# Low parts of the gates' inputs on VectorE, six branches' products with the state on GpSimd, another order of units, and another start, in a decoder trunk on one core

## The chip, the cores and the metric

The kernel runs on one core of a Trainium2 chip. The metric is the device time of one execution in microseconds (us); the kernel before takes 1247.46 us, the median of three runs between 1246.99 and 1248.34.

The engines are called TensorE (PE in the profile; its weight loads are PEld), VectorE (DVE), ScalarE (ACT), GpSimd (POOL) and SyncE (SP), which issues nearly all loads. Each engine works through its own instructions strictly in their order.

## The reference, cut to what matters

The trunk has two layers over 512 prompt tokens and 8 x 8 sample tokens, width 1024. Layer 0 is the recurrent block; the rest of the kernel (two feed-forward parts, shared keys and values, sliding attention, final norm) isn't touched.

```python
sh1, sc1, g1, ... = split(silu(c) @ ada_w + ada_b)          # modulation, from the condition c
h = rms_norm(x, g) * (1 + sc1) + sh1
xr, yg = split(h @ w_in)                                    # two branches, 8 blocks of 128 each
xr = causal_dwconv(xr, conv_buf, conv_w, conv_b)            # width 4
r, i = sigmoid(einsum(xr blocks, gate_w) + gate_b)          # the gates, block by block
a = exp(8 * r * log_sigmoid(lambda))
state_t = a * state_(t-1) + sqrt(1 - a * a) * (i * xr)      # the scan over the tokens
out = (state * gelu(yg)) @ w_out
x = x + g1 * out
```

## The kernel before, in words

**Tokens and blocks.** The tokens are two halves h of 288 columns (256 prompt and 32 sample tokens). Feature blocks c of 128 lie on the partitions. A product with a weight of 128 x 1024 is 8 blocks, and each block is three matmuls, because every operand is held as a high part (rounded to fp32r) and a low part (the rest): high x high, high x low, low x high. Raw weights come by DMA into `raw` tiles; ScalarE casts the high part and VectorE subtracts for the low part, both into `wh` tiles.

**The recurrent block.** The string `RNN` lists its units: `x3` is the branch that is convolved for block 3 (`evac_xr`), `g3` its gates (`gates`), `y3` its gelu branch (`evac_yg`). In `gates`, ScalarE casts the convolved input to its high part (tile `ta`), and line 1180 takes the low part (tile `tb`): 128 x 300, by GpSimd. Six matmuls follow (two gates, three each); the tanh and exp of ScalarE, five products of VectorE and a scan of VectorE then give the state in `s0`. GpSimd puts start values into the scan's operands (`ta<-shT`, `sl<-tb`, a memset) and copies ends out (`ho`). In `evac_yg`, ScalarE takes gelu, VectorE multiplies by the state (lines 1244 and 1245: 256 prompt columns, then 32 sample columns), ScalarE casts the high part, VectorE takes the low part; both wait as `sl` tiles for the product with `w_out`.

**What sets the order.** The code doesn't issue instructions itself. A `Recorder` writes every operation down with its operands, and `schedule` (line 235) then places all of them on the five engines, with a planned cost for each, and emits them in the order of the planned starts. So a change of one operation's engine or of a constant moves many rows, on every engine. That is also why all instructions have one line, L497, in the profile: it is the line that emits. `early(n)` makes what it encloses more urgent; `rec.hold` makes what follows wait for the writers of a tile.

**The start.** SyncE loads x (five tiles of rows, `reg`), the conditions c (`raw`), two vectors and then weights. `x_half` takes the sums of squares, whose by-product goes to spare `raw` tiles, and turns x with transposes. `keep_busy` offers 60 transposes of the unit matrix to TensorE for the time in which it would have nothing to do. `more_vectors` loads eight small vector groups from GpSimd's queue, `vectors_rest` turns them with four transposes. `lambdas` turns the decay parameters, and `decay_rates` makes two tiles (`sp`, `nsp`) from them with some 27 small operations of GpSimd, placed after the block pair `DKC`. `ada_first` makes the first modulation in four steps of two blocks, each from 2 MB of `ada_w`.

Of the kernel before, what the change touches and what calls it, by code (L numbers as in the profile page):

```python
# [15 lines left out]
AF = mybir.ActivationFunctionType  # L16
ALU = mybir.AluOpType
AX = mybir.AxisListType

P = 128  # L20
D = 1024
# [5 lines left out]
HP = 256  # L27
HC = 288
CW = 300
# [26 lines left out]
QUAD = (3, 4, 5, 6)  # L56
QK = 2
YT = lambda td, ta, sl: td
RNN = "x0 x1 x2 x3 x4 x5 g0 g1 y0 y1 g2 x6 g3 y2 y3 g4 y4 g5 x7 y5 g6 g7 y7 y6"
ATT = "q0A q2A a0A q1A q0B a2A q1B q3A a0B q2B q4A a1A a1B a4A a3A q3B a2B q5A q4B a3B q6A a5A q5B q7A a6A a4B s0A a5B s1A s2A s3A q6B q7B a7A s0B s1B a6B fA a7B o0A s2B s3B o1A o2A fB"  # L60
LOOK = {"PE": 24, "DVE": 24, "ACT": 24, "POOL": 24, "SP": 24}
NRAW = 4
FILL = 250
DKC = 2
XB = 100
AF_ = (1, 2, 2, 2)
NSL, NTA, NTB, NTD = 37, 7, 8, 4


SH1, SC1, G1, SH2, SC2, G2 = range(6)  # L70
# [68 lines left out]
class Recorder:  # L139
# [95 lines left out]
    def schedule(self):  # L235
# [22 lines left out]
        pos = {n: j for k in self.order for j, n in enumerate(self.order[k])}  # L258
        used = {n for n in last}
        table = [next(j for j, (n, _) in enumerate(TABLES) if n == "silu")]  # L260
        dma_free = [0.0]
        out = []

        def push(op):
# [35 lines left out]
        while n_left:  # L300
# [24 lines left out]
            for e in engs:  # L325
# [4 lines left out]
                for pr, i, op in avail[e]:  # L330
# [13 lines left out]
                    s = max(f, op.ready, at)  # L344
                    if op.port == 1:
                        s = max(s, port - 100 + (60 if holder == e else 0))
                    if e == "PE" and op.mode != mode:
                        s = max(s, f + 100)
# [19 lines left out]
            _, s, op, sw = best  # L368
# [24 lines left out]
            if op.lat:  # L393

                free[e] = s + op.cost
                b = max(s + op.cost + 650, dma_free[0])
                dma_free[0] = b + op.lat
                op.end = b + op.lat + (1700 if op.i >= self.strict else 1000)
            else:
                op.end = free[e] = s + cost  # L400
            for n in op.tiles:
# [122 lines left out]
def trunk_kernel(ctx, tc, a):  # L524
# [17 lines left out]
    def aux():  # L542
        return ps()
# [36 lines left out]
    @contextmanager  # L580
    def early(n):

        rec.bias -= n
        yield
        rec.bias += n
# [10 lines left out]
    v1, v2, v3, v4, v5, v6 = [s.f[:, 0:P] for s in vb]  # L596
    lam_ = sl()
    lam = lam_.f[0:8, 0:P]
    G.dma_start(lam, a["rnn_lambda"][0].rearrange("(r p) -> r p", p=P))

    def first_vectors():
        Q.dma_start(v1[0:96, :], a["ada_b"].rearrange("l (r p) -> (l r) p", p=P))
        Q.dma_start(v6[0:32, :], a["norm_g"].rearrange("l n (r p) -> (l n r) p", p=P))

    def more_vectors():
        G.dma_start(v2[64:80, :], a["kv_ada_b"].rearrange("(r p) -> r p", p=P))
        G.dma_start(v2[0:8, :], a["kv_norm_g"].rearrange("(r p) -> r p", p=P))
        G.dma_start(v2[8:40, :], a["rnn_conv_w"][0].rearrange("w (r p) -> (w r) p", p=P))
        G.dma_start(v2[40:48, :], a["rnn_conv_b"][0].rearrange("(r p) -> r p", p=P))
        G.dma_start(v2[48:64, :], a["rnn_gate_b"][0].rearrange("n (r p) -> (n r) p", p=P))  # L610
        G.dma_start(v3[0:96, :], a["state_conv"][0, 0:4].rearrange("b w (r p) -> (b w r) p", p=P))
        G.dma_start(v4[0:96, :], a["state_conv"][0, 4:8].rearrange("b w (r p) -> (b w r) p", p=P))
        G.dma_start(v5[0:64, :], a["state_h"][0].rearrange("b (r p) -> (b r) p", p=P))

    more_vectors()

    xt = [None] * 5

# [2 lines left out]
    def x_load(t):  # L621
        xt[t] = regs()
        if t < 4:
            Q.dma_start(xt[t].f, a["x_prompt"][0, t * P : (t + 1) * P, :])
        else:
            Q.dma_start(xt[t].f[0:64, :], a["x_sample"].rearrange("b t d -> (b t) d"))
# [17 lines left out]
        xt[t].done()  # L644

    S.activation(tst[1][:, 3:4], ones, AF.Silu)
    x_load(4)
    Q.dma_start(c9.f[0:1, :], a["c_prompt"])
    Q.dma_start(c9.f[1:9, :], a["c_sample"])
    for t in (0, 1):  # L650
        x_load(t)
    first_vectors()


    for q in range(2):
        S.activation(cst[q], cst[q], AF.Silu)
    pt = aux()
    for k in range(KC):
        T.transpose(pt[:, k * 16 : k * 16 + 9], cst[k // 4][:, (k % 4) * P : (k % 4) * P + P], ident[0:9, 0:9])
# [38 lines left out]
    def lambdas():  # L698
        pt = aux()
        T.transpose(pt[:, 0:8], lam, ident[0:8, 0:8])  # L700
        V.tensor_copy(lamT, pt[:, 0:8])
        lam_.done()
# [140 lines left out]
    def v48(t):  # L843
        return t.rearrange("p (b t) -> p b t", b=4)
# [329 lines left out]
    def gates(c):  # L1174
        def run(h):
            s1 = RN[h][c]
            xc = s1.f[:, 0:CW]
            xh, xl = ta(F32R), tb(F32R)
            S.copy(xh.r[:, 0:CW], xc)
            G.tensor_tensor(xl.r[:, 0:CW], xc, xh.f[:, 0:CW], ALU.subtract)  # L1180
            os_ = []
            for t in range(2):
                o = ps()[:, 0:CW]
                hi, lo = ug[c // 4].block(c % 4 * 2 + t)
                T.matmul(o, hi, xh.r[:, 0:CW], start=True, stop=False)
                T.matmul(o, lo, xh.r[:, 0:CW], start=False, stop=False)
                T.matmul(o, hi, xl.r[:, 0:CW], start=False, stop=True)
                os_.append(o)
            xh.done()
            xl.done()  # L1190

            s0, sa = sl(), sl()
            RN[h][c] = s0
            r_, i_ = ta(), tb()
            r, i, t, b = [y.f[:, 0:CW] for y in (r_, i_, s0, sa)]
            S.activation(r, os_[0], AF.Tanh, bias=hgb[:, 2 * c : 2 * c + 1], scale=0.5)
            S.activation(i, os_[1], AF.Tanh, bias=hgb[:, 2 * c + 1 : 2 * c + 2], scale=0.5)
            S.activation(t, r, AF.Tanh, bias=sp2[:, c : c + 1], scale=sp2[:, c : c + 1])
            S.activation(b, r, AF.Exp, bias=nsp4[:, c : c + 1], scale=nsp4[:, c : c + 1])
            V.scalar_tensor_tensor(xc, i, 1.0, xc, ALU.add, ALU.mult)  # L1200
            S.activation(r, t, AF.Sqrt)
            V.scalar_tensor_tensor(i, b, 1.0, t, ALU.add, ALU.mult)
            V.scalar_tensor_tensor(r, r, 0.5, xc, ALU.mult, ALU.mult)
            V.scalar_tensor_tensor(r, b, 1.0, r, ALU.add, ALU.mult)
            G.tensor_scalar(b, i, -1.0, 1.0, ALU.mult, ALU.add)
            G.memset(pads(b), 0.0)
            G.tensor_copy(pads(r), shT[:, 4 * h : 4 * h + 4, c])
            V.tensor_tensor_scan(t, b, r, 0.0 if h == 0 else ho5[:, 0, c, 0:1], ALU.mult, ALU.add)
            r_.done()
            i_.done()  # L1210
            s1.done()
            sa.done()
            G.tensor_copy(ho5[:, h, c], s0.f[:, 249:304].rearrange("p (b t) -> p b t", t=11)[:, :, 6])
        return run
# [23 lines left out]
    def evac_yg(c):  # L1238
        def f(h, o):
            s0 = RN[h][c]  # L1240
            t = YT(td, ta, sl)()
            v = t.f[:, 0:HC]
            S.activation(v, o[:, 0:HC], AF.Gelu_apprx_tanh)
            V.tensor_tensor(v[:, 0:HP], v[:, 0:HP], s0.f[:, 0:HP], ALU.mult)
            V.tensor_tensor(v48(v[:, HP:HC]), v48(v[:, HP:HC]),
                            s0.f[:, 259:303].rearrange("p (b t) -> p b t", t=11)[:, :, 0:8], ALU.mult)
            RN[h][c] = sl(F32R), sl(F32R)
            split(RN[h][c][0].r[:, 0:HC], RN[h][c][1].r[:, 0:HC], v)
            s0.done()
            t.done()  # L1250
        return f
# [285 lines left out]
    def keep_busy(t, n):  # L1537
        with rec.when_idle():
            for i in range(n):
                T.transpose(t[:, 0:P], ident[:], ident[:])  # L1540
# [426 lines left out]

    def x_half(h):
        st = tst[h]
        for t in ((4, 0, 1), (2, 3))[h]:  # L1970

            w = raws()
            n, y = (64, tst[1][0:64, 2:3]) if t == 4 else (P, st[:, t % 2 : t % 2 + 1])
            src, dst = xt[t].f[0:n, :], w.f[0:n, :]
            if t % 2 == 0:
                S.activation(dst, src, AF.Square, accum_out=y)
            else:
                V.tensor_tensor_reduce(out=dst, in0=src, in1=src, op0=ALU.mult, op1=ALU.add, scale=1.0, scalar=0.0, accum_out=y)
            w.done()
            if t == 4:  # L1980
                V.tensor_scalar(tst[0][0:32, 2:3], y[0:32], 1.0 / D, EPS, ALU.mult, ALU.add)
                V.tensor_scalar(tst[1][32:64, 2:3], y[32:64], 1.0 / D, EPS, ALU.mult, ALU.add)
        V.tensor_scalar(st[:, 0:2], st[:, 0:2], 1.0 / D, EPS, ALU.mult, ALU.add)
        spread(h, 32 * h)
        for t in ((4, 0, 1), (2, 3))[h]:
            x_turn(t)


    keep_busy(aux(), 60)
    lambdas()  # L1990
    def load_one():
        load_more(nload[0] - nconv[0] + 1)

# [17 lines left out]
    for c in range(0, KC, 2):  # L2011
        ada_first(c, AF_[c // 2])
        for h in range(2):
            with early(E1):
                modulated(h, SC1, SH1, M1, slice(c, c + 2))
            if c + 2 == QK:
                quad_parts(h)
            if c == 0 and h == 0:
                with early(XB):
                    x_half(1)  # L2020
                rec.idle_end()
        if c == DKC:
            decay_rates()
    vectors_rest()
    first_norm[0] = False
# [130 lines left out]
```

## Time and profile before

| | |
|---|---|
| median of the runs | 1247.46 us |
| the profiled execution | 1247.53 us |
| its span | 1245.8 us |
| TensorE busy in the span | 1232.7 us, 9603 matmul records |
| VectorE, ScalarE, GpSimd busy | 895.3, 655.5, 461.9 us |
| loads | 160.85 MB read, 133 GB/s over the span |

The span runs from the first to the last instruction of the trace; the time has 1.7 us around it. A row of the timeline gives the start and the length in us, engine, line, operation, output<-input and shape, how many instructions are merged in it, and in brackets how long the engine had idled before and on what. A row of a group gives the number of instructions, their busy time in us and the mean of one in ns. A row of the waits gives the total, how often, and the longest.

### The profile page before, as it was taken

Reading aid. Unit: us, or ns where it says so; the run is one execution under the profiler, and the core shown is the slowest. Engines: PE = TensorE matmul, PEld = TensorE weight load, DVE = VectorE, ACT = ScalarE, POOL = GpSimd, SP = SyncE. Lnnn points to the kernel's source line nnn. Section 1 sums busy time; section 2 is a strip of 40 time slices with the busy share of each in tenths; the row PEclk is TensorE's granted clock in tenths of the full one; section 3 lists DMA queues with packets and bytes.
Section 4 is the critical chain, followed back from the end, with each engine's and each line's share of the span. In section 5 each row is a group of like instructions: output and inputs, shape, how many; then the busy total and the mean of one; then the engine's idle time right before and its main releaser. Section 6 shows DMA issues by size and latency. Waiting matters only on the chain.

```text
span 1245.8 us, 25395 instructions
## 1 busy us (share of the span) xinstructions
PE 1232.7 (99%) x9603; PEld 1171.4 (94%) x9603; DVE 895.3 (72%) x2141; ACT 655.5 (53%) x1462; POOL 461.9 (37%) x633
## 2 busy tenths in 40 slices
PE   8999999999999999999999999999999999999997
PEld 7888899999999999999999988999999999999997
DVE  5997885896675676477578888568767667747766
ACT  6778863852452454145367678448425435515533
POOL 4464340162441452246125445100426246335500
PEclk9999999999999999999999999999999999999999
DMA  9984644326556555444433321422332323323222
GB/s 317 298 266 162 197 150 153 124 73 216 170 184 203 172 169 166 162 145 155 119 88 69 72 61 41 122 75 99 98 105 69 110 78 102 102 83 87 84 87 77
DMA packets 221117, 165.41 MB, mean 133 GB/s; under 512 B 23757, under 2 KB 206025, under 8 KB 220962
## 3 DMA queue, kind: packets, MB, share of 16 engines
q1 hardware_dynamic: 220514, 163.45, 42.6%
q8 instruction: 76, 1.25, 0.4%
q14 instruction: 47, 0.39, 0.1%
q0 software_dynamic: 480, 0.32, 0.1%
HBM read 160.85 MB, written 4.87 MB: 133 GB/s over the span
## 4 chain that ended last, share of the span: by engine, by line
PE 94%; DMA 2%; DVE 2%; POOL 1%; ACT 1%; SPq 0%; issue 0%; DVEq 0%; POOLq 0%; ACTq 0%
PE mm L497 89%; PE ada L497 5%; DMA reg<-in_x_prompt_dram 1%; DVE wh L497 1%; DMA wh<-in_ada_w_dram 0%; DMA raw<-in_ffn_w_out_dram 0%; POOL tb L497 0%; SPq L497 0%; DVE ta L497 0%; DVE h L497 0%; POOL sl L497 0%; DMA wh<-in_cache_k_dram 0%; DVE tb L497 0%; ACT wh L497 0%; POOL ta L497 0%
## 5 line engine op out<-in xcount | busy, mean ns | idle before, releaser
L497 PE MATMUL mm<-h,wh 128*128 128x288 f32 x4080 | 583.5, 297 | 0.9 <-DVE h L497 0.4
L497 PEld LDWEIGHTS mm<-h,wh 128*128 128x128 f32 x4080 | 552.8, 188 | 11.2 <-issue 6.4
L497 PE MATMUL mm<-sl,wh 128*128 128x288 f32 x3237 | 464.6, 296 | 0.2 <-ACT sl L497 0.2
L497 PEld LDWEIGHTS mm<-sl,wh 128*128 128x128 f32 x3237 | 440.0, 188 | 6.8 <-issue 5.9
L497 ACT CAST wh<-raw 128x512 fp32r<-128x512 f32 (+3 forms) x394 | 270.6, 706 | 293.4 <-PE mm L497 182.9
L497 DVE TENSOR_TENSOR wh<-raw,wh 128x512 fp32r<-128x512 f32 (+3 forms) x396 | 360.5, 930 | 54.1 <-ACT wh L497 48.6
L497 POOL TENSOR_TENSOR raw<-raw 128x512 f32<-128x512 f32 x78 | 114.5, 1469 | 174.9 <-DVE wh L497 157.4
L497 DVE SCALAR_TENSOR_TENSOR x<-mm,mods,x 128x256 f32<-128x256 f32 x160 | 77.2, 483 | 122.8 <-PE mm L497 122.1
L497 POOL TENSOR_TENSOR x<-x,ta 128x32 f32<-128x32 f32 x120 | 42.1, 351 | 243.4 <-DVE ta L497 243.4
L497 POOL TENSOR_TENSOR raw<-raw,raw 128x512 f32<-128x512 f32 x78 | 116.1, 1488 | 4.6
L497 PE MATMUL mm<-tb,wh 128*128 128x288 f32 (+1 forms) x500 | 92.0, 299 | 2.4 <-POOL tb L497 2.4
L497 POOL TENSOR_TENSOR td<-td,td 128x288 f32<-128x288 f32 x39 | 32.7, 837 | 134.8 <-ACT td L497 121.7
L497 PEld LDWEIGHTS mm<-tb,wh 128*128 128x128 f32 x500 | 73.9, 188 | 6.3 <-POOL tb L497 2.9
L497 ACT ACTIVATE ta<-x 128x288 f32<-128x288 f32 (+1 forms) x56 | 24.4, 442 | 62.8 <-POOL x L497 39.9
L497 PE MATMUL mm<-ta,wh 128*128 128x288 f32 (+1 forms) x259 | 56.7, 296 | 0.0
L497 DVE TENSOR_TENSOR td<-mm,td 128x288 f32<-128x288 f32 x78 | 34.4, 453 | 22.7 <-PE mm L497 21.9
L497 PE MATMUL ada<-reg,cz 128*32 128x512 f32 (+1 forms) x408 | 47.2, 547 | 0.0
L497 DVE TENSOR_TENSOR sl<-td,sl 128x288 fp32r<-128x288 f32 x65 | 41.5, 642 | 7.9 <-ACT sl L497 7.6
L497 PEld LDWEIGHTS mm<-ta,wh 128*128 128x128 f32 x259 | 42.3, 188 | 1.0 <-ACT sl L497 0.8
L497 ACT ACTIVATE td<-td 128x288 f32<-128x288 f32 x39 | 17.3, 443 | 46.1 <-DVE td L497 46.1
L497 ACT ACTIVATE ta<-ta,stat 128x256 f32<-128x256 f32 (+2 forms) x72 | 32.5, 473 | 11.0 <-DVE stat L497 10.7
L497 ACT COPY ta<-mm 128x288 f32<-128x288 f32 (+1 forms) x51 | 19.1, 377 | 36.3 <-PE mm L497 35.2
(212 smaller groups left out, 1243.1 us busy)
## 6 DMA issues: line engine op xcount, KB each, us to landing
raw<-in_ffn_w_in_dram SPq DMA_DIRECT2D x88, 512.0 KB
reg<-in_ada_w_dram SPq DMA_DIRECT2D x72, 512.0 KB
raw<-in_ffn_w_out_dram SPq DMA_DIRECT2D x32, 384.0 KB
raw<-in_ffn_w_out_dram SPq DMA_DIRECT2D x32, 320.0 KB
reg<-in_kv_ada_w_dram SPq DMA_DIRECT2D x14, 512.0 KB
raw<-in_rnn_w_in_dram SPq DMA_DIRECT2D x13, 512.0 KB
wh<-in_ada_w_dram SPq DMA_DIRECT2D x24, 256.0 KB
raw<-in_rnn_w_out_dram SPq DMA_DIRECT2D x8, 512.0 KB
```

The costliest lines, as they stand in the source:

```text
L497: self.rec.add(eng, lambda: getattr(obj, name)(*map(real, args), **{k: real(v) for k, v in kw.items()}), cost, outs, ins, func, lat, port, ...
```

## The change: what it does

In `gates`, the low part of the input (line 1180) goes from GpSimd to VectorE: 16 operations of 128 x 300. In `evac_yg`, the products with the state of blocks 0 to 5 go from VectorE to GpSimd: 12 products of 256 columns and 12 of 32. The order of units in `RNN` is another. At the start: x tile 0 is loaded first instead of the samples; the eight vector groups and the decay parameters are loaded after the first modulation is written (`rec.hold`), not at once; the decay rates are made after the block pair 4 instead of 2; the by-product of the first squares goes into x of the other half; ScalarE gets one more early table load. In `schedule`, two planned costs of DMAs are others.

```diff
-RNN = "x0 x1 x2 x3 x4 x5 g0 g1 y0 y1 g2 x6 g3 y2 y3 g4 y4 g5 x7 y5 g6 g7 y7 y6"
+RNN = "x0 x1 x2 x3 x4 x5 g0 g1 y0 g2 y1 g3 y3 y2 x6 g4 x7 g5 y4 y5 g6 g7 y7 y6"
...
-DKC = 2
+DKC = 4
...
+NFILL = 60
+YG = 6
+OFF = 3000.0
...
-        dma_free = [0.0]
+        dma_free = [OFF]
...
+                if e == "POOL":
+                    op.end = s + op.cost + 5000
...
-    G.dma_start(lam, a["rnn_lambda"][0].rearrange("(r p) -> r p", p=P))
...
     def more_vectors():
+        G.dma_start(lam, a["rnn_lambda"][0].rearrange("(r p) -> r p", p=P))
...
-    more_vectors()
...
-    x_load(4)
+    x_load(0)
     Q.dma_start(c9.f[0:1, :], a["c_prompt"])
     Q.dma_start(c9.f[1:9, :], a["c_sample"])
-    for t in (0, 1):
-        x_load(t)
+    x_load(1)
+    x_load(4)
...
+    with early(1000):
+        S.activation(tst[0][:, 3:4], ones, AF.Sqrt)
...
-            G.tensor_tensor(xl.r[:, 0:CW], xc, xh.f[:, 0:CW], ALU.subtract)
+            V.tensor_tensor(xl.r[:, 0:CW], xc, xh.f[:, 0:CW], ALU.subtract)
...
-            V.tensor_tensor(v[:, 0:HP], v[:, 0:HP], s0.f[:, 0:HP], ALU.mult)
-            V.tensor_tensor(v48(v[:, HP:HC]), v48(v[:, HP:HC]),
+            E = G if c < YG else V
+            E.tensor_tensor(v[:, 0:HP], v[:, 0:HP], s0.f[:, 0:HP], ALU.mult)
+            E.tensor_tensor(v48(v[:, HP:HC]), v48(v[:, HP:HC]),
...
-            w = raws()
+            r = raws() if h else None
+            w = r.f if h else x[1].rearrange("p c n -> p (c n)")[:, D * (t % 2) : D * (t % 2 + 1)]
...
-    keep_busy(aux(), 60)
-    lambdas()
+    keep_busy(aux(), NFILL)
...
+                rec.hold = [mods[:, SC1, 0:2]]
+                more_vectors()
+                rec.hold = []
         if c == DKC:
+            lambdas()
             decay_rates()
```

TensorE, the start, before: the transposes of the unit matrix (`mm2`) stand between the others as they are planned. `reg1` is the sample tile, `reg2` and `reg3` are x tiles 0 and 1, `raw1` the conditions, `sl7` the decay parameters.

```order
L497 MATMUL mm2_99<-ident_66 128x128 x25
L497 MATMUL mm3_139<-ident_66,sl7_94 128x8
L497 MATMUL mm2_99<-ident_66 128x128 x2
L497 MATMUL mm5_149<-ident_66,reg1_97 128x64 x8
L497 MATMUL mm2_99<-ident_66 128x128 x7
L497 MATMUL mm1_179<-ident_66,raw1_105 128x9 x8
L497 MATMUL mm6_195<-ident_66,reg2_118 128x128 x4
```

TensorE, the same place after: here `reg1` and `reg2` are x tiles 0 and 1 and `reg3` is the sample tile.

```order
L503 MATMUL mm2_97<-ident_66 128x128 x50
L503 MATMUL mm4_178<-ident_66,reg1_94 128x128 x4
L503 MATMUL mm5_184<-ident_66,reg1_94 128x128 x4
L503 MATMUL mm2_97<-ident_66 128x128 x5
L503 MATMUL mm6_203<-ident_66,reg2_123 128x128
L503 MATMUL mm1_205<-ident_66,raw1_111 128x9 x8
```

50 of the 60 fillers now stand in a block at the front; 60 are planned in both. Further down, the turning of the decay parameters and of the vectors (`sl2` to `sl5`) has left the start and stands around the second step of the first modulation (`ada26` is its transpose, `ada27` the third step), after:

```order
L503 MATMUL ada26_586<-ident_66,ta8_536 128x128
L503 MATMUL mm32_588<-ident_66,sl2_352 128x80
L503 MATMUL mm33_590<-ident_66,sl3_431 128x96
L503 MATMUL mm33_590<-ident_66,sl4_446 128x96
L503 MATMUL mm33_590<-ident_66,sl5_461 128x64
L503 MATMUL ada27_601<-reg6_294,cz_78 32x128 x8
```

The same place before, where the third step follows at once:

```order
L497 MATMUL ada27_630<-ident_66,ta8_570 128x128
L497 MATMUL ada28_632<-reg6_324,cz_78 32x128 x8
L497 MATMUL ada28_632<-reg7_343,cz_78 32x128 x8
L497 MATMUL mm38_661<-h11_508,wh5_362 128x288
L497 MATMUL ada28_632<-reg8_355,cz_78 32x128 x8
```

What moved is four transposes, from a place among the fillers to one where the third step's modulation is due.

TensorE, a gate of the recurrent block, before: `ta47` is the high part of the input, `tb41` its low part, `mm74` and `mm76` other units.

```order
L497 MATMUL mm72_1797<-ta47_1779,wh27_1019 128x300
L497 MATMUL mm72_1797<-ta47_1779,wh28_1177 128x300
L497 MATMUL mm73_1803<-ta47_1779,wh27_1019 128x300
L497 MATMUL mm73_1803<-ta47_1779,wh28_1177 128x300
L497 MATMUL mm74_1808<-h01_375,wh41_1786 128x288 x2
L497 MATMUL mm72_1797<-tb41_1792,wh27_1019 128x300
L497 MATMUL mm73_1803<-tb41_1792,wh27_1019 128x300
```

TensorE, the gate of the same place after:

```order
L503 MATMUL mm72_1813<-ta47_1736,wh29_1133 128x300
L503 MATMUL mm72_1813<-ta47_1736,wh30_1149 128x300
L503 MATMUL mm72_1813<-tb41_1789,wh29_1133 128x300
L503 MATMUL mm73_1824<-ta47_1736,wh29_1133 128x300
L503 MATMUL mm73_1824<-ta47_1736,wh30_1149 128x300
L503 MATMUL mm73_1824<-tb41_1789,wh29_1133 128x300
```

The third matmul, which takes the low part, no longer stands behind matmuls of other units.

ScalarE, the first two gelu branches (`td11` and `td14`), after. The casts of `td11` and `td14` follow GpSimd's products, and tanh of gates (`ta36`, `ta38`) stand behind the casts:

```order
L503 ACTIVATE td11_1436<-mm49_1244 128x288
L503 ACTIVATE ta34_1442<-mm51_1330,hgb_81 128x300
L503 ACTIVATE tb30_1450<-mm52_1338,hgb_81 128x300
L503 ACTIVATE sl34_1457<-ta34_1442,sp2_79 128x300
L503 ACTIVATE td14_1463<-mm54_1382 128x288
L503 CAST sl31_1470<-td11_1436 128x288
L503 ACTIVATE ta36_1476<-mm55_1387,hgb_81 128x300
L503 ACTIVATE tb32_1482<-mm56_1460,hgb_81 128x300
L503 ACTIVATE sl39_1491<-ta36_1476,sp2_79 128x300
L503 CAST sl37_1501<-td14_1463 128x288
L503 ACTIVATE ta38_1505<-mm57_1467,hgb_81 128x300
```

Before, the same branches with the products by VectorE (`td11` and `td13`):

```order
L497 ACTIVATE td11_1359<-mm49_1249 128x288
L497 ACTIVATE td13_1386<-mm51_1340 128x288
L497 CAST ta37_1399<-sl22_1065 128x300
L497 CAST wh35_1411<-raw18_1191 128x768
L497 CAST sl31_1426<-td11_1359 128x288
L497 ACTIVATE ta34_1431<-mm53_1408,hgb_81 128x300
L497 ACTIVATE sl36_1440<-td14_1328,vecT_73 128x300
L497 CAST sl34_1453<-td13_1386 128x288
```

The two products stand one behind the other in GpSimd's queue now. The last 7826 of TensorE's 9034 matmuls stand in the same order in both kernels: the rows differ up to the first columns of the product with `w_out`.

More of the change, by code (lines that the diff above doesn't have):

```diff
@@ L395, in schedule @@
                 free[e] = s + op.cost
-                b = max(s + op.cost + 650, dma_free[0])
-                dma_free[0] = b + op.lat
-                op.end = b + op.lat + (1700 if op.i >= self.strict else 1000)
+                if e == "POOL":
+                    op.end = s + op.cost + 5000
+                else:
+                    b = max(s + op.cost + 650, dma_free[0])
+                    dma_free[0] = b + op.lat
+                    op.end = b + op.lat + (1700 if op.i >= self.strict else 1000)
             else:
@@ L1969, in x_half @@
         st = tst[h]
-        for t in ((4, 0, 1), (2, 3))[h]:
-            w = raws()
+        for t in ((0, 1, 4), (2, 3))[h]:
+            r = raws() if h else None
+            w = r.f if h else x[1].rearrange("p c n -> p (c n)")[:, D * (t % 2) : D * (t % 2 + 1)]
             n, y = (64, tst[1][0:64, 2:3]) if t == 4 else (P, st[:, t % 2 : t % 2 + 1])
-            src, dst = xt[t].f[0:n, :], w.f[0:n, :]
+            src, dst = xt[t].f[0:n, :], w[0:n, :]
             if t % 2 == 0:
@@ L1978, in x_half @@
                 V.tensor_tensor_reduce(out=dst, in0=src, in1=src, op0=ALU.mult, op1=ALU.add, scale=1.0, scalar=0.0, accum_out=y)
-            w.done()
+            if h:
+                r.done()
             if t == 4:
@@ L1984, in x_half @@
         spread(h, 32 * h)
-        for t in ((4, 0, 1), (2, 3))[h]:
+        for t in ((0, 1, 4), (2, 3))[h]:
             x_turn(t)
-    keep_busy(aux(), 60)
-    lambdas()
+    keep_busy(aux(), NFILL)
     def load_one():
```

## The prediction

> **What bounds the kernel now.** I read the page's first part, then who TensorE waited for, then TensorE's timeline where those waits lie.
>
> ```profile
> span 1245.8 us, 25395 instructions
> PE 1232.7 (99%) x9603; PEld 1171.4 (94%) x9603; DVE 895.3 (72%) x2141; ACT 655.5 (53%) x1462; POOL 461.9 (37%) x633
> ```
>
> TensorE is busy for 1232.7 of 1245.8 us. The order shows as many matmuls in both kernels, so at most the 13.1 us of its idle time, and what its 60 fillers cover, can change. The profiled execution took 1247.53 us, 0.07 from the median of 1247.46; I work against 1247.53. A measurement of this kernel can tell about 0.2% from no change: 2.5 us.
>
> ```profile
> PE mm L497 <- POOL tb L497: 2.4, 2, 1.7
> PE mm L497 <- POOL few L578: 1.4, 1, 1.4
> PE mm L497 <- DMA reg<-in_x_prompt_dram: 1.3, 1, 1.3
> PE mm L497 <- DVE h L497: 0.4, 1, 0.4
> PE mm L497 <- DVE wh L497: 0.4, 1, 0.4
> ```
>
> These five rows are 5.9 of the 13.1 us; most of the rest is the kernel's end, whose order the change leaves as it is. The first row is the change's target: `tb` is the low part of a gate's input. The third to fifth lie in the start. The timeline places them:
>
> ```profile
> 18.98 1.09 PE L497 MATMUL mm<-ident,reg 128*128 128x128 f32 x8 [1.30 <-DMA reg<-in_x_prompt_dram]
> 21.57 2.55 PE L497 MATMUL mm<-h,wh 128*128 128x288 f32 x16
> 24.50 1.33 PE L497 MATMUL mm<-h,wh 128*128 128x288 f32 x8 [0.39 <-DVE wh L497]
> 36.27 1.87 PE L497 MATMUL mm<-h,wh 128*128 128x288 f32 x12 [0.41 <-DVE h L497]
> ...
> 110.46 0.41 PE L497 MATMUL mm<-tb,wh 128*128 128x300 f32 x1 [0.69 <-POOL tb L497]
> ...
> 119.13 0.55 PE L497 MATMUL mm<-tb,wh 128*128 128x300 f32 x2 [1.69 <-POOL tb L497]
> ```
>
> After 36.27 TensorE has no gap up to 110, so a gain or a loss made ahead of 36 is passed on whole, and 0.69 + 1.69 = 2.38 us is all that the gates can give.
>
> **Term 1: the gates' low parts go to VectorE.** Sixteen operations leave GpSimd. Why the two came late:
>
> ```profile
> L497 POOL TENSOR_TENSOR tb<-sl,ta 128x300 fp32r<-128x300 f32 x16 | 20.4, 1282 | 12.5 <-ACT ta L497 9.2 <-PE mm L497 3.1 <-issue 0.3
> 89.41 0.83 POOL L497 TENSOR_TENSOR tb<-sl,ta 128x300 fp32r<-128x300 f32 x1 [3.72 <-ACT ta L497]
> 115.57 3.51 POOL L497 TENSOR_TENSOR tb<-sl,ta 128x300 fp32r<-128x300 f32 x1 [3.06 <-PE mm L497]
> 115.67 1.22 DVE L497 TENSOR_TENSOR wh<-raw,wh 128x1024 fp32r<-128x1024 f32 x1
> 116.80 0.47 DVE L497 SCALAR_TENSOR_TENSOR sl<-tb,sl 128x300 f32<-128x300 f32 x1
> 117.19 1.22 DVE L497 TENSOR_TENSOR wh<-raw,wh 128x1024 fp32r<-128x1024 f32 x1
> ```
>
> Undisturbed it takes 0.83 us; at 115.57 it took 3.51, for as long as VectorE ran three operations with two inputs, and the wait of 1.69 us ended with it. On VectorE no row shows the operation with 300 columns; the nearest has 288:
>
> ```profile
> L497 DVE TENSOR_TENSOR sl<-td,sl 128x288 fp32r<-128x288 f32 x16 | 8.0, 515 | 1.1 <-ACT sl L497 1.0
> L497 DVE TENSOR_TENSOR td<-td,sl 128x256 f32<-128x256 f32 x16 | 6.4, 409 | 0.1
> L497 DVE TENSOR_TENSOR td<-td,sl 128x32 f32<-128x32 f32 x16 | 3.5, 234 | 0.0
> 40.00:60.00 20.00, 20.00 (x199) 17.56 (x198) 19.68 (x66) 15.40 (x37) 6.85 (x15) 1.00 0.89 286
> 60.00:80.00 20.00, 20.00 (x154) 18.39 (x151) 19.76 (x39) 14.42 (x25) 15.35 (x20) 1.00 0.91 291
> ```
>
> So VectorE gets 16 x 0.52 = 8.2 us and gives back 12 x (0.41 + 0.23) = 7.7 us: level in sum. But the early low parts come in the stretch where VectorE is busy for 19.68 and 19.76 of 20 us (third of the engine figures), and the products that it gives back come only behind 80. Queued behind a low part on VectorE are the convolutions and the low halves of weights. The first pair of low parts now stands behind one more 1024-wide low half than the matmul that needs it can easily wait for; counting VectorE's rows there by their durations I find its end within half a us of TensorE's need. Bounds: no wait (VectorE also loses its partner in the contention above), or the first two low parts late by their own 2 x 0.52 plus one 1.22, 2.3 us. I take 0.6, nearer to none, since TensorE had no wait for VectorE there in spite of 99% busy. Term 1: -2.38 + 0.6 = -1.8 us.
>
> **Term 2: products on GpSimd, another order of units.** Twelve products of 256 and twelve of 32 columns go to GpSimd; the nearest rows:
>
> ```profile
> 14.93 1.63 POOL L497 TENSOR_TENSOR ta<-x,acc 128x256 f32<-128x256 f32 x2 [7.68 <-ACT acc L497]
> L497 POOL TENSOR_TENSOR x<-x,ta 128x32 f32<-128x32 f32 x10 | 4.9, 488 | 25.6 <-DVE ta L497 25.6
> L497 ACT ACTIVATE tb<-mm,hgb 128x300 f32<-128x300 f32 x16 | 8.2, 515 | 0.0
> ```
>
> A branch costs 1.63 / 2 + 0.49 = 1.3 us there against 0.64 on VectorE. Behind it wait ScalarE's cast, and behind that, for the first two branches, tanh of gates, which free PSUM. In the order, three tanh and a gelu stand between the first gelu and its cast; at the 0.52 us of the last row they take some 2 us, which covers 1.3 and leaves 0.7. For four later branches more stands between. A scan of VectorE can also wait, where GpSimd's start values queue behind a product. I take 0 for this term if GpSimd isn't blocked; a block costs 3.51 - 0.83 = 2.7 us less the 0.7 of cover, 2.0 each. The other order of units only changes which work covers what.
>
> [...]
>
> **Term 3: the start.** The fillers: 25 at the front now, 14 later on.
>
> ```profile
> 1.44 4.93 PE L497 MATMUL mm<-ident 128*128 128x128 f32 x25 [1.44 <-POOL few L578]
> 6.30 0.22 PE L497 MATMUL mm<-ident,sl 8*128 8x8 f32 x1
> 11.12 1.75 PE L497 MATMUL mm<-ident 128*128 128x128 f32 x14
> 14.34 0.29 PE L497 MATMUL mm<-ident,sl 80*128 80x80 f32 x1
> 15.62 0.25 PE L497 MATMUL mm<-ident,sl 96*128 96x96 f32 x1
> 17.44 0.25 PE L497 MATMUL mm<-ident,sl 96*128 96x96 f32 x1
> ```
>
> The first 25 take 0.197 us each, later ones 0.125. Fifty in a block end at about 1.44 + 4.93 + 25 x 0.125 = 9.5; the turning of x and conditions and the first modulation follow as before, and by the same rows its last transpose comes at 17.1 as it did. So the block costs nothing; x tiles 2 and 3 may land up to 0.7 us sooner without the vectors' loads, but what follows them needs the first normalised blocks and their low parts, which hang on that modulation and on VectorE: the row at 21.57 moves by 0.3 at most, the one at 24.50 by 0.4.
>
> Against that, four transposes (0.22 + 0.29 + 0.25 + 0.25, 1.0 us, their ends overlapping, so I take 0.8) leave the time of the fillers and come behind 27, where TensorE has work. One more stood behind 18.98 already. And VectorE's copies of them now stand ahead of the third step's normalised blocks:
>
> ```profile
> 14.66 0.17 DVE L497 COPY abT<-mm 128x16 f32<-128x16 f32 x1 [1.39 <-PE mm L497]
> 14.76 0.21 DVE L497 COPY vecT<-mm 128x64 f32<-128x64 f32 x1
> 24.89 0.36 DVE L497 COPY scv<-mm 128x192 f32<-128x192 f32 x1
> 34.01 1.47 POOL L497 TENSOR_TENSOR ta<-x,acc 128x256 f32<-128x256 f32 x2
> 34.11 0.76 DVE L497 TENSOR_TENSOR tb<-tb,mods 128x64 f32<-128x64 f32 x1
> 34.79 0.97 DVE L497 TENSOR_TENSOR h<-tb,h 128x256 fp32r<-128x256 f32 x1
> ```
>
> 0.17 + 0.21 + 0.36 = 0.74 us on the path that made TensorE wait 0.41 us at 36.27. The transposes fill that time in part. One of GpSimd's two operations that stretched VectorE there comes earlier now, which gives up to half a us back. Sum: -0.4 + 0.8 + 0.74 - 0.5 (the gap filled) - 0.25 = +0.4 us, between -0.6 (all cover holds) and +1.5 (none). The decay rates' operations move to about 46, beside GpSimd's old low parts' time, and are needed behind 70: nothing. The table load is ScalarE's in front of its first data: nothing.
>
> **Sum.** 1247.53 - 1.8 + 0 + 0.4 = 1246.1 us.
>
> **The rivals.** *A clean gain.* No low part is late on VectorE, and the start gives 0.6: 1247.53 - 2.38 - 0.6 = 1244.6. For it: VectorE's contention with GpSimd's low parts goes. Against it: the moved transposes are real work. *VectorE in GpSimd's place.* The low parts wait in the full queue: 2.3 us instead of 0.6, so 1247.8. For it: 99% busy; against it: the waits of before lie behind 100, where VectorE has room. *The vectors land late.* GpSimd's loads are issued from about 18, among VectorE's work.
>
> ```profile
> sl<-in_state_h_dram POOLq DMA_DIRECT2D x1, 32.0 KB, 5.8
> ```
>
> The last landed 5.8 us after its issue; nine issues at half a us put it at 29, four ahead of need. If it comes at 35, TensorE stops for 2 us: 1248.1. [...] *Slower: products blocked.* GpSimd's products meet VectorE's bursts of weight halves, the casts come late, tanh behind them too, and TensorE finds no free PSUM. One block makes 1246.1 + 2.0 = 1248.1; from two it is slower than before clearly, 1250.1; three make 1252.1. For it: the row at 115.57. Against it: twelve products, of which only the first two have little cover, and in the waits TensorE never stood for PSUM.
>
> That the change doesn't do what it says is excluded for the engines by the order; for the start it is the +1.5.
>
> **How the numbers follow.** The forecast has 0.46, the clean gain 0.20, VectorE in GpSimd's place 0.13, late vectors 0.07, blocked products 0.14. The first, third and fourth lie within 2.5 us of 1247.46: 0.66. Faster by more: 0.20; slower by more: 0.14. I predict 1246.1; with its terms at their ends it could be 1244.6 to 1249.0. The range reaches down to the clean gain with both gaps of 0.4 us in the start gone as well, 1243.8, and up to two blocked products, 1250.1; three blocks and more are left out.
>
> **What would show it.** Right: no wait of TensorE for `tb` of GpSimd; under 1 us in sum for `tb` of VectorE between 60 and 75; the matmuls at 36.27 begin within 1 us of it; no waits for PSUM behind 80. Wrong: a wait for GpSimd's `td` through ScalarE, GpSimd's products at 2 us or more on the way to it; a start later by over 1.5; a gap at the vectors' transposes; or new gaps behind 180, where the order is the same.

## The result, and the profile after

The changed kernel takes 1245.94 us (median, 1244.69 to 1247.42) against 1247.70 of the kernel before on the same chip: ratio 0.9987, 95% interval 0.9981 to 0.9993. It is 1.8 us faster: the interval leaves out 1, but the gain is less than the 2.5 us (0.2%) that the prediction counts as a difference. The forecast was 1246.1. The profiled execution took 1246.18 us, its span is 1244.4 us.

The page's first part, and who TensorE waited for, after:

```profile
PE 1231.8 (99%) x9603; PEld 1171.7 (94%) x9603; DVE 893.8 (72%) x2133; ACT 657.7 (53%) x1464; POOL 462.6 (37%) x641
PE mm L503 <- DVE tb L503: 1.4, 2, 0.8
...
PE mm L503 <- DMA reg<-in_x_prompt_dram: 1.2, 1, 1.2
PE mm L503 <- DVE wh L503: 0.6, 1, 0.6
PE ada L503 <- ACT ta L503: 0.4, 1, 0.4
```

The 2.4 us for `tb` of GpSimd are gone; 1.4 us for `tb` of VectorE stand in their place. TensorE's timeline after, at the start and at those two waits:

```profile
17.72 0.33 PE L503 MATMUL ada<-ident,ta 128*128 128x128 f32 x1 [0.39 <-ACT ta L503]
19.26 1.06 PE L503 MATMUL mm<-ident,reg 128*128 128x128 f32 x8 [1.21 <-DMA reg<-in_x_prompt_dram]
25.14 1.59 PE L503 MATMUL mm<-h,wh 128*128 128x288 f32 x10 [0.61 <-DVE wh L503]
36.01 1.20 PE L503 MATMUL mm<-h,wh 128*128 128x288 f32 x4
58.42 1.92 PE L503 MATMUL ada<-reg,cz 128*32 128x512 f32 x16
70.14 0.54 PE L503 MATMUL mm<-tb,wh 128*128 128x300 f32 x2 [0.79 <-DVE tb L503]
137.06 0.41 PE L503 MATMUL mm<-tb,wh 128*128 128x300 f32 x1 [0.67 <-DVE tb L503]
186.40 1.92 PE L503 MATMUL ada<-reg,cz 128*32 128x512 f32 x16
1236.58 0.61 PE L503 MATMUL mm<-ident,x 128*128 128x128 f32 x3
```

Four rows of before show how late the same matmuls were there:

```profile
17.09 0.29 PE L497 MATMUL ada<-ident,ta 128*128 128x128 f32 x1
58.12 1.93 PE L497 MATMUL ada<-reg,cz 128*32 128x512 f32 x16
187.01 1.92 PE L497 MATMUL ada<-reg,cz 128*32 128x512 f32 x16
1237.95 0.61 PE L497 MATMUL mm<-ident,x 128*128 128x128 f32 x3
```

At 58 the changed kernel is 0.3 us behind: the start. At 187, behind all that the change touches, it is 0.61 ahead, and that adds up: +0.3 - 2.38 + 1.46 = -0.62. At the end it is 1.37 ahead. The other 0.76 us came in a stretch where both kernels have the same order and neither shows a wait that the other lacks. They aren't shown to come from the change: between the four transposes near 189 and the last three, the fourteen profiled executions of this document took 1047.18 to 1048.92 us, and none waits there for more than 0.34 us. The shortest is the changed kernel with more fillers, from 190.19 to 1237.37.

The second new wait isn't the full queue of the forecast. The chain of waits after, ahead of 137 (start, length, what):

```profile
130.47 1.83 POOL td L503 x2
132.32 0.43 ACT sl L503
132.77 1.28 ACT L503
134.06 0.71 ACT td L503 x2
134.78 0.40 ACT ta L503
135.17 0.41 ACT tb L503
135.61 0.04 DVE sl L503
135.99 1.02 DVE tb L503
```

GpSimd's products (`td`) hold up ScalarE's cast (`sl`), a table load, gelu and tanh stand behind it, VectorE waits for tanh with the low part queued behind, and the low part then takes 1.02 us beside more products. Up to tanh this is the chain of the rival "products blocked"; it ends in VectorE's low part, not at PSUM, and costs 0.67 us here.

### The profile page after: what moved, and what is told of

Its sections match the earlier page's. It is cut to its first block, busy times and chain, and to the rows that moved or that the text cites. A ratio compares the mean times of both kernels' runs of the same rounds, so it can differ in the third digit from the quotient of the medians.

```text
span 1244.4 us, 25387 instructions
## 1 busy us (share of the span) xinstructions
PE 1231.8 (99%) x9603; PEld 1171.7 (94%) x9603; DVE 893.8 (72%) x2133; ACT 657.7 (53%) x1464; POOL 462.6 (37%) x641
## 3 DMA queue, kind: packets, MB, share of 16 engines
q8 instruction: 76, 1.25, 0.4%
## 4 chain that ended last, share of the span: by engine, by line
PE 91%; DVE 3%; DMA 2%; ACT 1%; POOL 1%; issue 1%; SPq 0%; DVEq 0%; ACTq 0%
PE mm L503 86%; PE ada L503 5%; DVE sl L503 1%; DVE wh L503 1%; POOL sl L503 1%; DMA raw<-in_rnn_w_in_dram 1%; ACT sl L503 1%; DVE tb L503 1%; DMA wh<-in_ada_w_dram 1%; DVE h L503 0%; DMA raw<-in_ffn_w_out_dram 0%; DVE ta L503 0%; SPq L503 0%; ACT L503 0%; ACT ta L503 0%
## 5 line engine op out<-in xcount | busy, mean ns | idle before, releaser
L503 ACT ACTIVATE td<-td 128x288 f32<-128x288 f32 x39 | 17.3, 443 | 46.7 <-DVE td L503 46.7
```

The costliest lines, as they stand in the source:

```text
L503: self.rec.add(eng, lambda: getattr(obj, name)(*map(real, args), **{k: real(v) for k, v in kw.items()}), cost, outs, ins, func, lat, port, ...
```

## The experiments

Theory "low parts": the gain is the removed wait less the new ones and the start, as summed above. Rivals: the order of units, the products, the start. All medians are beside the kernel before on the same chip (1247.63, 1247.87 and 1247.72 us in the three groups of four). The intervals are about 1 us to either side, so a difference of half a us between two variants is a hint only; where variants of different groups are compared, each is taken against the kernel before in its own group.

**Low parts back on GpSimd.**

```diff
-            V.tensor_tensor(xl.r[:, 0:CW], xc, xh.f[:, 0:CW], ALU.subtract)
+            G.tensor_tensor(xl.r[:, 0:CW], xc, xh.f[:, 0:CW], ALU.subtract)
```

> The changed kernel with the gates' 16 low parts back on GpSimd; products, order of units and start stay changed. Theory 'low parts': the changed kernel lost 2.4 us of waiting for GpSimd's tb and gained 1.4 us of waiting for VectorE's; so here TensorE waits again for tb of GpSimd, 2 to 4 us in sum (GpSimd now also has the products), none for tb of VectorE, and the time is 1246.9 to 1248.5, about that of the kernel before. Rival 'units': the waits went because the units stand in another order, whatever the engine; then under 0.5 us of waiting for GpSimd's tb and 1245.5 or less.

Measured: 1245.42 us, ratio 0.9987 (0.9978 to 0.9995). The row of TensorE's waits for `tb`:

```profile
PE mm L503 <- POOL tb L503: 0.3, 1, 0.3
```

The wait for GpSimd's `tb` is 0.3 us, with the engine as before. Theory "low parts" falls: in this order of units the engine of the low parts decides nothing that can be measured.

**All products on VectorE.**

```diff
-YG = 6
+YG = 0
```

> The changed kernel with all products with the state on VectorE. Theory 'low parts': the products did nothing for the gain, and the second new wait for tb (0.67 us at 137), whose low part ran beside GpSimd's products, is gone; 1245.0 to 1245.6, the first new wait (0.8 us at 70) stays. Rival 'relief': VectorE only has room for the low parts because the products left it; then the waits for VectorE's tb grow beyond 2 us in sum and the time is 1246.5 to 1248.

Measured: 1247.2 us, 0.9997 (0.9988 to 1.0006). Unclear against either theory: the wait at 137 is gone and only one for `tb`, of 0.8 us, is left, as "low parts" said, yet the time is the one that "relief" gave. VectorE's group of low parts in it:

```profile
L503 DVE TENSOR_TENSOR tb<-sl,ta 128x300 fp32r<-128x300 f32 x16 | 7.0, 460 | 0.0
```

Its profiled execution was 0.5 us ahead of the changed kernel's at 187 and lost 0.6 us from there to the last transposes, in the stretch that varies by more than that from trace to trace. That doesn't explain a median over eleven runs; what makes this kernel 1.3 us slower than the changed one stays open. The row shows that without products on GpSimd a low part takes 0.46 us on VectorE; the changed kernel's mean is 0.515.

**The start of before**, with low parts, products and units of the changed kernel. The edit undoes all other lines of the change (loads, decay rates, fillers, table load, planned DMA costs).

> The start, the planned DMA costs and the decay rates of the kernel before, with low parts, products and units of the changed one. Theory 'low parts': the changed start costs 0.3 us (TensorE's ada transpose at 58.42 against 58.12), so 1245.3 to 1245.9, and no wait for GpSimd's tb. Rival 'start': the gain comes from the start; then 1247.2 to 1247.8.

Measured: 1246.28 us, 0.9990 (0.9981 to 0.9999), runs from 1245.92 to 1246.97. That is between the two expectations, 0.4 us above that of "low parts"; with 1.35 of the 1.8 us still there, the start isn't the gain. The wait at 70 is gone and the one at 137 stays:

```profile
136.55 0.41 PE L498 MATMUL mm<-tb,wh 128*128 128x300 f32 x1 [0.67 <-DVE tb L498]
```

**The changed start alone**, on gates, products and units of before.

```diff
-            V.tensor_tensor(xl.r[:, 0:CW], xc, xh.f[:, 0:CW], ALU.subtract)
+            G.tensor_tensor(xl.r[:, 0:CW], xc, xh.f[:, 0:CW], ALU.subtract)
...
-YG = 6
+YG = 0
...
-RNN = "x0 x1 x2 x3 x4 x5 g0 g1 y0 g2 y1 g3 y3 y2 x6 g4 x7 g5 y4 y5 g6 g7 y7 y6"
+RNN = "x0 x1 x2 x3 x4 x5 g0 g1 y0 y1 g2 x6 g3 y2 y3 g4 y4 g5 x7 y5 g6 g7 y7 y6"
```

> The changed start alone, on the gates, products and units of the kernel before. Theory 'low parts': 0.3 us above the kernel before, 1247.7 to 1248.3, with the waits for GpSimd's tb still 2 to 3 us in sum. Rival 'start': 1245.9 to 1246.5.

Measured: 1247.3 us, 0.9998 (0.9989 to 1.0007). The start gains nothing by itself that can be measured. But even here no matmul waited for GpSimd's `tb`. The profiled execution, the slowest of the eleven with 1249.71 us, waits 2.4 us for an x tile at the start (first row); in the gates there are two waits for gelu instead (second row):

```profile
PE mm L503 <- DMA reg<-in_x_prompt_dram: 2.4, 1, 2.4
PE mm L503 <- ACT td L503: 1.8, 2, 1.2
```

So a change far from the gates, which lets the planned order fall out otherwise, removes the wait as well.

**Units and start alone** (low parts on GpSimd, `YG = 0`, the changed `RNN`).

> Changed start and changed order of units; low parts on GpSimd and products on VectorE as before. Theory 'products' (that GpSimd has the products is what brought the gain, since all products on VectorE cost the changed kernel 1.3 us, and low parts back on GpSimd cost nothing): 1246.9 to 1247.6. Rival 'units' (the order of units removed the waits): 1245.2 to 1246.0.

Measured: 1246.47 us, 0.9989 (0.9981 to 0.9998). It lies between the two expectations; no matmul waits for `tb`, and of the gates' region 0.62 us for gelu (`td`) and 0.24 us are left as waits. Against the start alone the order of units is worth 1.1 us without any move between engines, which is a hint, since the intervals overlap.

**Products alone on the changed start** (low parts on GpSimd, `YG = 6`, `RNN` of before).

> Changed start and products on GpSimd; low parts on GpSimd and order of units as before. Theory 'products': 1245.2 to 1246.0, with under 0.7 us of waiting for GpSimd's tb in spite of the 28 operations that GpSimd has in the gates. Rival 'units': 1247.0 to 1248, with waits for GpSimd's tb or for what hangs on its products.

And **the units of before**: the changed kernel with `RNN` of before, nothing else undone.

> The changed kernel with the order of units of before. Theory 'products': 0.3 to 0.6 us above the products alone, since the low parts on VectorE only cost, so 1245.7 to 1246.4. Rival 'units': 1247.2 or more.

Measured: 1253.88 us, 1.0048 (1.0034 to 1.0061), and 1252.57 us, 1.0039 (1.0026 to 1.0051). Theory "products" falls too, by far. The second kernel is the changed one but for the order of units, and it is 6.5 us slower. Its timeline has one new wait in the gates, and the chain of waits ahead of it shows why:

```profile
142.61 0.86 PE L503 MATMUL mm<-ta,wh 128*128 128x300 f32 x2 [4.00 <-ACT td L503]
```

```profile
137.84 0.49 POOL td L503
138.33 1.13 POOL ho L503
139.46 0.92 POOL td L503
...
140.40 0.43 ACT sl L503
...
140.85 1.28 ACT L503
142.15 0.42 ACT td L503
```

GpSimd's products (`td`) stand between its copies of the scan's ends (`ho`), which wait for VectorE's scan; ScalarE's cast (`sl`) waits for the last product; a table load and gelu (`td`), which frees PSUM, stand behind the cast; TensorE stands for 4.00 us. With the changed order of units a like chain costs 0.67 us. Not all of the 6.5 us belong to the units: this trace is 1.18 us behind the changed kernel's at 58 already, because its start was slower, and 6.44 us at 189, so some 5.3 us come in between. In the first kernel no single wait is that long: between 139 and 146 five of 1.56, 0.24, 0.61, 0.63 and 0.35 us follow each other, for gelu, tanh and GpSimd's `tb`.

**Products and changed units on the start of before**, low parts on GpSimd.

> The kernel before with products on GpSimd and the changed order of units; low parts on GpSimd and the start of before. If those two bring the gain whatever the start: 1245.5 to 1246.0, no wait for GpSimd's tb over 0.5 us, and runs within 1 us of each other, as the runs with the start of before were. If the two waits of before for GpSimd's tb went because of the changed start (with it alone the trace had none): they are here again, 1 to 3 us in sum, and 1246.8 to 1248.

Measured: 1255.98 us, 1.0068 (1.0056 to 1.0081), runs from 1255.76 to 1257.69. Worse than either expectation.

It has eight waits between 88 and 176, 7.4 us in sum; these are the two longest, and GpSimd's rows ahead of the second:

```profile
113.58 3.43 PE L498 MATMUL mm<-h,wh 128*128 128x288 f32 x24 [2.18 <-DVE mods L498]
175.85 0.54 PE L498 MATMUL mm<-tb,wh 128*128 128x300 f32 x2 [2.27 <-POOL tb L498]
```

```profile
172.85 1.96 POOL L498 TENSOR_TENSOR td<-td,sl 128x256 f32<-128x256 f32 x2
174.77 1.03 POOL L498 TENSOR_TENSOR tb<-sl,ta 128x300 fp32r<-128x300 f32 x1
```

Here the low part that TensorE waits for at 175.85 stood behind two products in GpSimd's queue (second fence). The wait at 113.58 hangs on VectorE, which makes the low half of a weight first. With the low parts on VectorE the same kernel took 1246.28 (the start of before, above), with the changed start and low parts on GpSimd 1245.42. So products and low parts on GpSimd together give the lowest median of all or the highest, and the two kernels differ in the start alone, with the order that follows from it. That makes a third theory, "order": where the planned order puts units decides which waits there are, and an engine's move acts above all by changing that order.

**Low parts alone on the kernel before.**

```diff
-            G.tensor_tensor(xl.r[:, 0:CW], xc, xh.f[:, 0:CW], ALU.subtract)
+            V.tensor_tensor(xl.r[:, 0:CW], xc, xh.f[:, 0:CW], ALU.subtract)
```

> The kernel before with the gates' 16 low parts on VectorE, nothing else changed in the program. The first theory's term 1 by itself: the two waits for GpSimd's tb (2.4 us) go, new ones for VectorE's tb take 0.6 to 1.4 us, so 1245.8 to 1246.9. Theory 'order': the moved work lets the planned order fall out otherwise, and waits appear that have nothing to do with tb; anything between 1246 and 1252, with the waits of the profile naming other tiles.

Measured: 1248.83 us, 1.0009 (1.0000 to 1.0018). No matmul waits for `tb` any more, of either engine, and the kernel is 1.1 us slower:

```profile
138.18 0.87 PE L497 MATMUL mm<-ta,wh 128*128 128x300 f32 x2 [2.42 <-ACT td L497]
```

```profile
138.00:139.00 1.00, 0.82 (x3) 0.57 0.95 283
139.00:140.00 1.00, 1.00 (x6) 0.50 1.04 373
140.00:141.00 1.00, 1.00 (x6) 0.50 0.98 391
141.00:142.00 1.00, 1.00 (x8) 0.72 1.11 343
```

The chain of waits ahead of 138.18, in part:

```profile
131.60 2.10 DVE sl L497 x3
...
135.38 0.51 DVE sl L497
...
136.43 1.28 ACT L497
...
137.72 0.42 ACT td L497
```

The wait removed, 2.38 us, came back as a wait of 2.42 us for gelu, and behind it the granted clock (the fifth column of the second fence's rows, after TensorE's busy time and its count) fell to half. The missing shares, 0.43 + 0.50 + 0.50 + 0.28, make 1.7 us by estimate. The rows agree: the 18 matmuls of 300 columns from 138.18 took 4.10 us up to the next row, and 9 like them from 86.02, at a clock of 1.00, took 1.25, so 1.6 us were lost. That fits theory "order", but a rival fits too, the load: the chain is VectorE's from 127.8 to 135.9, and VectorE, which has the low parts now, is busy for 18.57 of the 20 us from 120 to 140, where it was 16.40 before. No run tells the two apart here; in the changed order VectorE takes the same low parts at no price that can be measured.

**More fillers.** The same fall of the clock was in the start of four profiled executions with the changed start. Of units and start alone, the timeline at the place and the windows of TensorE behind it:

```profile
17.46 0.33 PE L503 MATMUL ada<-ident,ta 128*128 128x128 f32 x1 [0.39 <-ACT ta L503]
19.45 1.48 PE L503 MATMUL mm<-ident,reg 128*128 128x128 f32 x8 [1.66 <-DMA reg<-in_x_prompt_dram]
```

```profile
19.00:20.00 1.00, 0.55 (x5) 0.97 1.03 395
20.00:21.00 1.00, 1.00 (x7) 0.50 1.05 371
21.00:22.00 1.00, 1.00 (x6) 0.50 1.06 330
22.00:23.00 1.00, 1.00 (x7) 0.50 1.10 359
23.00:24.00 1.00, 1.00 (x8) 0.82 1.10 351
```

In the kernel before, fillers stood around the first of these two rows; in the changed one they are at the front, TensorE idles twice, and from 20 its clock is 0.50. The changed kernel's own profiled execution, with 0.39 and 1.21 us, shows 1.00 there. Three kernels got 80 instead of 60, with nothing else moved:

```diff
-NFILL = 60
+NFILL = 80
```

The changed kernel:

> The changed kernel with 80 fillers instead of 60; nothing else moves. The 20 new ones stand between 14 and 19, 7 of them behind the first modulation's transpose at 17.7, where TensorE otherwise stands until x tile 2 has landed. Theory 'clock': in executions in which that tile lands late, TensorE idles for about 2 us in all around 18 and its granted clock then falls to 0.5 until 23, which costs 1.7 us and spreads the changed kernel's runs over 2.7 us. Then here the runs lie within 1.3 us, no run shows a clock of 0.996 or less, and the median is 1245.3 to 1245.8. Rival 'landing': the spread is the tile's landing alone; the runs spread over 2 us or more and the median is 1245.8 or higher (the fillers delay the modulation by up to 1 us).

With low parts on GpSimd:

> The changed kernel with low parts back on GpSimd, and with 80 fillers. With 60 fillers it took 1245.42, its slower runs those with a lower clock. Theory 'clock': 1245.1 to 1245.5, runs within 1.3 us. If the low parts on VectorE gained 0.5 us or more by themselves, it is above the changed kernel with 80 fillers by that; if they only cost, below it by 0.2 to 0.6.

With units and start alone:

> Changed start and changed units, 80 fillers, low parts on GpSimd and products on VectorE as before: neither move between engines. Theory 'order': what removed the two waits for GpSimd's tb is where the planned order puts units, whatever the engines; then no wait for tb and 1245.1 to 1245.8, as fast as the changed kernel. Rival 'engines': without the two moves 1246.3 or more.

Measured: 1246.26 us (0.9980 to 0.9997), 1246.49 us (0.9982 to 1.0000) and 1246.82 us (0.9985 to 1.0003). The clock's mean over the execution was 0.998 or more in all 33 runs, where the changed kernel had 0.997 or less in 6 of 20; so the fillers seem to prevent the fall, and the traces have no wait for the x tile any more; yet no kernel with the changed start and 60 fillers ran on this chip. They don't pay: all three medians are above what theory "clock" gave, no run is below 1245.53, and the first modulation's transpose comes at 19.07 instead of 17.72:

```profile
19.07 0.29 PE L503 MATMUL ada<-ident,ta 128*128 128x128 f32 x1
```

The changed kernel's 14 runs at a clock of 0.998 or more have a median of 1245.62 us, its other 6 one of 1246.87; with low parts on GpSimd 1245.32 (8 runs) and 1246.71 (3), with units and start alone 1245.47 (5) and 1247.09 (6). So three kernels that share start and units and differ in the engines are within 0.3 us of each other where the clock held. The fourth is not: with all products on VectorE the six runs at such a clock have a median of 1247.13 us, so in the changed order low parts on VectorE without products on GpSimd look like the slow pairing. The groups were formed after the runs, so this too is a hint. With 80 fillers the kernel without engine moves is slowest, by 0.3 to 0.6 us, inside the intervals: it waits for no `tb`, as "order" said, but its time is the one that the rival "engines" gave.

## Why the prediction was right, and where it was not

*The time and the sign* were right: 1245.94 for 1246.1. That it came so close is luck in part: in the trace all that the prediction sums up makes -0.6 us and not the forecast -1.4, and 0.76 us more come from a stretch that the change doesn't touch. Of what would show it right, all four came: no wait for `tb` of GpSimd, 0.79 us for that of VectorE between 60 and 75, the matmuls of 36.27 at 36.01, no new gap for PSUM worth naming.

*Term 1* was nearly right in the trace and wrong as a cause. In the trace: the wait for VectorE's low part at 70 is 0.79 us where the forecast had 0.6, so -2.38 + 0.79 = -1.6 and not -1.8. As a cause: that the change of engine is what removes the wait fell with three kernels. Low parts alone remove it and are 1.1 us slower; low parts put back on GpSimd leave it removed; the start alone removes it as well. The wait belonged to one planned order.

*Term 2* was put at 0 and measured +0.67, the wait at 137: it hangs on GpSimd's products, for it stays with the start of before and goes with the products on VectorE. The term's working is wrong in one sentence: "The other order of units only changes which work covers what." Taken in pairs that differ in the order of units alone, the changed order is better by 1.1 us with products on VectorE (inside the intervals), and by 6.5 and 8.2 us with products on GpSimd (low parts on VectorE and on GpSimd). So the new order is the part of the change that helped in every pair, and without it the moved products cost far more than the low parts can give. The price of a block, 2.0 us, was too low: it left out what stands between cast and gelu (a table load of 1.28 us) and the clock's fall behind a long wait. (Of the "three tanh" that it counts as cover, one is an exp; the 2 us stand.) One block cost 4.00 us of waiting and, with the clock at 0.50 from 143 to 146, by estimate 1.7 us more (the two matmuls at 142.61 took 0.86 us, two like them in the changed kernel 0.44). The rival's chain was right from the cast on. What held the products there was in part another thing: they took 0.49 and 0.92 us and stood behind `ho` copies, one of which took 1.13 us while VectorE made the low half of a weight. The rival's chance of 0.14 stood for an order that the units' string had avoided.

*Term 3*, +0.4, measured +0.3 at 58. The step by which "the first modulation follow as before" failed: its last transpose came at 17.72 and not at 17.1, and with it the row at 24.50 came 0.64 later (25.14, with two matmuls more ahead of it), not 0.4 sooner. VectorE's copies cost no wait at 36, and the vectors landed in time: the last load, issued at 23.68, took 5.3 us, and their transposes began at 33.49. No trace showed a reason for them to land late. Not foreseen: the fillers gathered at the front leave TensorE idle behind 17.3, and the clock can fall there, 1.2 us between the two groups of the changed kernel's runs.

*What stays open*: 0.76 of the 1.37 us by which the profiled execution ended sooner lie in a stretch with the same order, without waits, which differs by up to 1.7 us between traces. A single execution can't say whether this belongs to a kernel or to the execution. What products on GpSimd are worth in the changed order isn't settled either: the pairs give 0.8 and 1.3 us with 60 fillers and 0.3 us with 80, all inside the intervals. No variant was measurably faster than the changed kernel.

## What to carry to other kernels

Where a scheduler lays out the order, removing a wait by moving an operation to another engine is half an edit: the order falls out anew, and the trace of before prices only the wait that goes. Before crediting the move, undo it alone and do it alone; here the wait stayed away in the one case and another, just as long, came in the other. An engine with room by its busy time isn't safe for an operation in a chain: look at what stands in its queue ahead of the operation and what stands behind its reader, down to what frees PSUM.

## What the runs showed of the hardware

TensorE's granted clock fell to 0.50 after waits of about 2 us and more, for some 3.4 us each: by the shares of the windows above, from 19.9 to 23.4 in units and start alone and from 138.1 to 141.6 in low parts alone. By estimate from these shares that costs 1.7 us on top of the wait; the rows of low parts alone make it 1.6. It fell at the start of four kernels (start alone, units and start alone, products alone on the changed start, units of before: mean clock of the profiled executions 0.997, 0.996, 0.994 and 0.995, the last two with the fall in the gates in them, against 0.998 for the other three with the changed start and 60 fillers), at 138 behind 2.42 us, at 142 behind 4.00 us, at 177 behind 2.27 us. With products alone on the changed start, the lowest of these means, it stayed at 0.50 for twice as long, from 142 to 148.8, amid and behind the five short waits. No sharp limit shows: idle times of 0.39 + 1.66 us around one transpose were enough at 18, and 2.18 us at 113.58 were not, with 0.43 us more ahead of four transposes.

The wait for the same x tile, loaded in the same order, was 0.2 to 2.4 us in the profiled executions with the changed start and 60 fillers. The changed kernel's 20 runs spread over 2.7 us, the 14 whose clock held over 2.3, where the 11 runs with the same gates on the start of before spread over 1.05; how much of that is the tile's landing no run shows.

The engines kept the program's order: in the changed kernel's trace the 2133 rows of VectorE and the 641 of GpSimd start in the order in which the program lists them.
